# Feed-forward of an encoder: another order of seven block products, early output products in six parts, token sums in four portions, returned operands asked for by thirds

## The chip, the core and the metric

The kernel runs on one core of one Trainium2 chip. The metric is the device time of one execution in microseconds, as the median of several runs. The core has a matrix engine (PE, with its weight loads shown as PEld), three engines for elementwise work (DVE is the vector engine, ACT the scalar engine, POOL the GpSimd engine), and DMA queues; here all loads and stores are issued from SP. Matrix products accumulate in PSUM, in banks of 128 x 512 numbers of 32 bits; everything else is in the on-chip SBUF.

## What is computed

Two layers over 512 tokens of width 1024. Each layer is a feed-forward, a token mixer (neighbourhood attention in the first layer, a bidirectional RWKV-7 scan in the second), and another feed-forward, each followed by a normalization:

```python
D_MODEL = 1024; SEQ = 512; DEPTH = 2; D_FF = 2816; DN_ALPHA = (2 * DEPTH) ** 0.25

def swiglu(x, w_in, w_out):
    gate, up = jnp.split(x @ w_in, 2, axis=-1)
    return (jax.nn.silu(gate) * up) @ w_out

for i in range(DEPTH):
    x = layer_norm(DN_ALPHA * x + 0.5 * swiglu(x, ffn_w_in[i, 0], ffn_w_out[i, 0]), ln_g[i, 0], ln_b[i, 0])
    m = neighbourhood_attention(...) if i % 2 == 0 else rwkv7_bidir(...)
    x = layer_norm(DN_ALPHA * x + m, ln_g[i, 1], ln_b[i, 1])
    x = layer_norm(DN_ALPHA * x + 0.5 * swiglu(x, ffn_w_in[i, 1], ffn_w_out[i, 1]), ln_g[i, 2], ln_b[i, 2])
```

The change is in the feed-forward, which runs four times with other weights.

## The kernel before

**Numbers in two parts.** Every operand of a matrix product is split into a high part (a copy on ACT, line 277, to a shorter format) and a low part (the difference, on DVE or POOL, line 278). A product is three matmuls: high by high, high by low, low by high. So each operand costs one ACT and one DVE or POOL instruction before PE can use it, and a wait of PE for "DVE w L278" is a wait for a low part.

**Blocks.** The inner width of 2816 is 22 blocks f of 128. `ffn()` goes through eleven pairs c, of the blocks f = 2c and 2c + 1. The even blocks, and those up to f = 4, are computed in the ordinary way: 24 matmuls of 512 columns for the gate (`pg`) and 24 for the up part (`pu`), lines 287 to 289, with a bank each; then a silu on ACT (L495) and a product on DVE that reads the bank of `pu` (L497). The odd blocks from f = 5 on (the list `SEVEN`, nine in each feed-forward, 36 in all) go through `Seven.products`.

**The seven products.** This is a Strassen scheme of Winograd's kind with the weights as a 2 x 2 block matrix (gate and up, first and second half of the width) and the tokens' transposed activations as another. `Seven.operands` makes the sums of weight blocks on DVE and splits them: `ua` and `ub` (in the tiles `w`, loaded from `raw`), `one` and `pair` (both in `ring` tiles; L957 and L958 make the sums ahead of these two splits). `Seven.mixes` makes the four sums of token blocks (`right`), once for each feed-forward. Each of the seven products is twelve matmuls of 256 columns (L980). They accumulate in three places: `a` and `f`, which are the two halves of one bank, and `e`, in half of the bank of the block before's `pu`. Partial results go between them by copies on ACT (L972): `copy(e, a)` from bank to bank, `copy(p, f)` to the tile `tmp`. PSUM dependencies are by tile, that is by bank: a matmul into `a` waits for a pending read of `f`, and the other way.

**The output side.** The second matrix is handled by the class `Winograd`. `sums(c)` loads four blocks of the output weights into `ra` (one buffer), makes differences (L1024 to L1027) and splits three of them into `wx`. `early(c - 1)` is a generator of output products X, Z and Y of the pair before, six matmuls of 512 columns each (L1063); `products` takes one part at a time between its own products, by `next(more)`. Of the other operands some (`keep`) stay in ring tiles, some are sent to DRAM (`away`) and returned by `recall`, three loads for each of two streams. When all pairs are done, streams V, Y, Z and Y (`add`) go over the pairs with 6 matmuls of 512 columns for each, with weights that are loaded and split on the way (tiles `w` and `wl`), while DVE adds finished accumulators to x (`more`, L531).

**What sets the order.** PE's order inside `products` is as written (manual schedule for PE); ACT, DVE and POOL are ordered by the scheduler of the framework, and each runs its queue strictly in that order. A wait at the head of a queue stops everything behind it on that engine. `k.behind(first[0])` lets the next product be issued after an instruction given. The tiles named `ring` come from a pool of 11 buffers.

Of the kernel before, what the change touches and what calls it, by code (L numbers as in the profile page):

```python
# [10 lines left out]
F32 = mybir.dt.float32  # L11
# [7 lines left out]
P = 128  # L19
D = 1024  # L20
# [86 lines left out]
class Trunk:  # L107
# [354 lines left out]
    def ffn(self, xT, w_in, w_out, ln, nxt, lead=None):  # L462
# [10 lines left out]
        with self.pool("fa") as pool:  # L473
            out.pool = pool
            keep = [self.ring().rearrange("p (c n i s) -> p c n i s", c=2, n=2, i=2) for _ in range(npairs // 2)]
            keep = [k[:, c] for k in keep for c in range(2)] + [seven.rest.rearrange("p (n i s) -> p n i s", n=2, i=2)]
            for c in range(npairs):
# [3 lines left out]
                for j in range(2):  # L481
# [10 lines left out]
                    if pps:  # L492
# [4 lines left out]
                        nc.vector.scalar_tensor_tensor(dst, halves_of(pu), 0.5, halves_of(s), ALU.mult, ALU.mult)  # L497
                    if f < 2:
                        seven.mixes(f)
# [7 lines left out]
                out.now[c] = pool.tile([P, 2, 3, 256], F32R, name="an", tag="an", bufs=1)  # L507
                self.split(out.now[c][:, 0], out.now[c][:, 1], raw[:, 0:3])
                self.split(keep[c][:, :, 0], keep[c][:, :, 1], raw[:, 3:5])
                tag = ("gbc", "bbc")[c % 2]  # L510
                away = self.home(self.sb).tile([P, 2, 2, 256], F32R, name="away", tag=tag)
                self.split(away[:, :, 0], away[:, :, 1], raw[:, 5:7])
                nc.sync.dma_start(self.away[:, :, c], away.bitcast(F32).rearrange("p n i s -> p n (i s)"))
            params = self.ln_params(ln)
            out.keep = {n: [k[:, n] for k in keep] for n in range(2)}
# [6 lines left out]
        with self.pool("fo") as pool:  # L522
            out.pool = pool
            out.begin(out.t3)
            out.recall(2)
            fin = self.residual_norm(params, nxt)
            hs = (slice(0, 512), slice(512, 1024))
# [16 lines left out]
            for t in (0, 1):  # L544
                more(t, 0, X, ALPHA)
                more(t, 0, V, 1.0, st[t][0])
            out.add("Y", 1, out.t3, range(npairs))
            out.begin(out.b22)
            out.recall(3)
            for t in (2, 3):  # L550
                more(t, 1, Y, 1.0, st[t][1])
            out.add("Z", 2, out.b22, range(npairs), lag=8)
            out.begin(out.t4)
# [337 lines left out]
class Seven:  # L891
# [21 lines left out]
    def mixes(self, part):  # L913

        nc, k = self.nc, self.k
        sub, add = ALU.subtract, ALU.add
        tt = nc.vector.tensor_tensor
        part_of = lambda b, i: b[:, i].bitcast(F32)
        x, y = (k.home(k.sb).tile([P, D], F32, name="mixed", tag=t).rearrange("p (c s) -> p c s", c=4) for t in ("gbc", "bbc"))

        def difference(out, t, a, b):
            tt(out, part_of(a, 0), part_of(b, 0), sub)
            tt(t, part_of(a, 1), part_of(b, 1), sub)
            tt(out, out, t, add)
# [8 lines left out]
        if part:  # L933
            difference(x, y, self.block(1, 1), self.block(0, 1))
            keep(2, x)
        else:
            difference(x, y, self.block(0, 1), self.block(0, 0))
            keep(0, x)
            fold(y, self.block(1, 1), x)
            keep(1, y)  # L940
            fold(x, self.block(1, 0), y)
            keep(3, x)

# [19 lines left out]
    def products(self, f, dst, more):  # L963
# [21 lines left out]
        b, t = self.block, self.right  # L985
        mul(a, ua[:, :, lo], b(0, 0), True)
        copy(e, a)
        next(more)
        with k.behind(first[0]):
            mul(f, ub[:, :, lo], t[0], False)  # L990
        copy(p, f)
        mul(e, self.one, t[1], False)
# [16 lines left out]
class Winograd:  # L1009
# [31 lines left out]
    def early(self, c):  # L1041

        a = self.now.pop(c)
        for name, n, u in zip("XYZ", (0, 2, 1), self.units.pop(c)):
            first = self.banks(name)
            for t in range(2):
                self.product(self.acc[name][t], a[:, :, n], t, u, first, c == NF // 2 - 1)
            yield

    def recall(self, n):  # L1050

        rings = [self.k.ring().rearrange("p (c f) -> p c f", c=4) for _ in range(3)]
        self.keep[n] = []
        for i, r in enumerate(rings):
            m = min(4, NF // 2 - 4 * i)
            self.nc.sync.dma_start(r[:, :m].bitcast(F32), self.k.away[:, n - 2, 4 * i : 4 * i + m])
            self.keep[n] += [r[:, c].rearrange("p (i s) -> p i s", i=2) for c in range(m)]

    def product(self, acc, a, t, u, first, last, more=False):
# [40 lines left out]

    def add(self, name, n, src, cs, lag=None):

# [934 lines left out]
```

## Time and profile before

| what | us |
|---|---|
| median of three runs (2205.87, 2219.66, 2207.17) | 2207.17 |
| the profiled execution, its own time | 2204.32 |
| its span in the trace | 2201.7 |
| mean granted clock of PE in it | 0.991 |

The four feed-forwards lie at about 36 to 345, 600 to 945, 945 to 1305 and 1845 to 2201 us of the span; attention and the scan lie between. The busy time of the engines in these stretches (columns: stretch, its length, then busy us and instructions of PE, PEld, DVE, ACT and POOL, granted clock, busy share of the DMA engines and GB/s):

```profile
36.00:345.00 309.00, 303.74 (x1680) 263.05 (x1679) 227.49 (x331) 141.84 (x210) 30.61 (x11) 1.00 0.58 196
600.00:945.00 345.00, 335.56 (x1905) 292.49 (x1904) 253.39 (x366) 159.32 (x236) 33.97 (x14) 1.00 0.52 180
945.00:1305.00 360.00, 352.67 (x2003) 308.24 (x2002) 269.25 (x396) 166.49 (x253) 49.88 (x22) 1.00 0.55 183
1845.00:2201.00 356.00, 337.73 (x1867) 290.01 (x1865) 257.19 (x373) 158.10 (x235) 30.84 (x12) 0.99 0.52 175
```

PE is busy nearly all the time in all four; DVE is the second. How to read the lines of the profile further on: a group shows engine, line, output and input by the program's names (buffer numbers left out), the shape, its busy time and mean, and the idle time ahead of it with what ended most of that. A line of the timeline shows the start, the duration, the instruction, and in brackets the engine's idle time before it with its releaser. Matmuls are pipelined, so their durations overlap; the pace is read from the starts.

### The profile page before, as it was taken

How to read it: one execution, taken by the hardware profiler on the slowest of the kernel's cores; microseconds unless marked ns; L12 is line 12 of the kernel's file. 1: busy time of each engine (PE TensorE's matmuls, PEld its weight loads, DVE VectorE, ACT ScalarE, POOL GpSimd, SP SyncE). 2: the span in 40 equal slices, each digit the busy share in tenths (PEclk: the TensorE clock that was granted, in tenths of full speed). 3: DMA queues.
4: the chain of work that ended last, by engine and by line, in shares of the span. 5: the costliest groups of instructions: out<-in, count | busy, mean ns of one | idle time of the engine just before them, and what ended most of it. 6: DMA issues, size and time to landing. Idle time of an engine off the chain costs nothing.

```text
span 2201.7 us, 38797 instructions
## 1 busy us (share of the span) xinstructions
PE 2131.1 (97%) x15248; PEld 1726.2 (78%) x15248; DVE 1551.5 (70%) x2506; ACT 1082.2 (49%) x1987; POOL 527.5 (24%) x670
## 2 busy tenths in 40 slices
PE   9999999999999999999999999999998999999998
PEld 8888888887888888787888877446666567788876
DVE  7777767377487777697777779636887558777775
ACT  4444445377344444453444444437776434444443
POOL 1000035555300000520000242046877610000023
PEclk9999999999999999999999999999999999999999
DMA  6544593432334556734555853853544551455583
GB/s 191 174 163 155 177 361 114 117 101 77 113 125 158 159 171 199 298 128 145 159 169 164 311 207 118 293 160 106 135 118 118 169 188 64 152 159 171 163 296 135
DMA packets 160805, 367.81 MB, mean 167 GB/s; under 512 B 32144, under 2 KB 52240, under 8 KB 158576
## 3 DMA queue, kind: packets, MB, share of 16 engines
q1 hardware_dynamic: 160624, 365.36, 50.9%
q8 instruction: 119, 1.95, 0.4%
q14 instruction: 62, 0.51, 0.1%
HBM read 284.29 MB, written 68.94 MB: 160 GB/s over the span
## 4 chain that ended last, share of the span: by engine, by line
PE 63%; DVE 18%; DMA 12%; ACT 3%; issue 2%; POOL 0%; SPq 0%; DVEq 0%; ACTq 0%; POOLq 0%
PE bank L980 13%; PE bank L1063 12%; DMA ra<-in_ffn_w_out_dram 7%; PE a L1255 5%; PE bank L288 5%; PE bank L287 5%; PE bank L289 5%; DVE w L278 4%; PE bank L350 4%; DVE ring L278 2%; ACT w L277 2%; DMA raw<-in_ffn_w_in_dram 2%; PE g L1579 1%; PE y L1255 1%; DVE wx L278 1%
## 5 line engine op out<-in xcount | busy, mean ns | idle before, releaser
L278 POOL TENSOR_TENSOR w<-raw,w 128x1024 fp32r<-128x1024 f32 x38 | 93.4, 2462 | 1206.5 <-ACT w L277 1200.2
L287 PE MATMUL bank<-xT,w 128*128 128x512 f32 x760 | 298.1, 392 | 6.5 <-DVE ar L497 6.5
L278 DVE TENSOR_TENSOR w<-raw,w 128x1024 fp32r<-128x1024 f32 x164 | 200.5, 1223 | 136.4 <-ACT w L277 134.6
L288 PE MATMUL bank<-xT,w 128*128 128x512 f32 x760 | 296.1, 390 | 0.0
L289 PE MATMUL bank<-xT,w 128*128 128x512 f32 x760 | 295.7, 389 | 0.0
L277 ACT ACTIVATE w<-raw 128x1024 fp32r<-128x1024 f32 x202 | 213.0, 1058 | 129.8 <-DMA raw<-in_ffn_w_in_dram 33.6
L1063 PE MATMUL bank<-wx,an 128*128 128x512 f32 x792 | 201.8, 392 | 0.0
L1063 PE MATMUL bank<-w,ring 128*128 128x512 f32 x720 | 171.8, 395 | 7.3 <-DVE w L278 7.3
L287 PEld LDWEIGHTS bank<-xT,w 128*128 128x128 f32 x760 | 142.7, 188 | 37.4 <-DVE ar L497 8.8
L277 ACT ACTIVATE ring<-raw 128x512 fp32r<-128x512 f32 (+1 forms) x99 | 89.3, 904 | 161.5 <-DVE raw L957 119.0
L1063 PEld LDWEIGHTS bank<-w,ring 128*128 128x128 f32 x720 | 136.7, 190 | 38.2 <-DVE w L278 9.0
L289 PEld LDWEIGHTS bank<-xT,w 128*128 128x128 f32 x760 | 142.7, 188 | 30.0
L288 PEld LDWEIGHTS bank<-xT,w 128*128 128x128 f32 x760 | 142.8, 188 | 28.4
L1063 PEld LDWEIGHTS bank<-wx,an 128*128 128x128 f32 x792 | 142.0, 189 | 24.7
L980 PEld LDWEIGHTS bank<-ring,w 128*128 128x128 f32 x864 | 110.8, 191 | 33.4 <-ACT bank L972 30.4
L980 PE MATMUL bank<-ring,w 128*128 128x256 f32 x864 | 119.0, 287 | 15.7 <-ACT bank L972 15.4
L1686 POOL TENSOR_TENSOR tm<-qs,zs 128x126 f32<-128x126 f32 (+22 forms) x248 | 102.8, 414 | 86.9 <-issue 38.9
L1688 POOL TENSOR_TENSOR zs<-zs,tm 128x126 f32<-128x126 f32 (+22 forms) x248 | 112.6, 454 | 19.4
L980 PE MATMUL bank<-ring 128*128 128x256 f32 x864 | 116.3, 284 | 0.1
L980 PEld LDWEIGHTS bank<-ring 128*128 128x128 f32 x864 | 109.6, 193 | 0.4 <-ACT tmp L972 0.4
L495 ACT ACTIVATE tmp<-bank 128x512 f32<-128x512 f32 x52 | 31.1, 597 | 151.8 <-PE bank L289 151.8
L980 PE MATMUL bank<-xT,w 128*128 128x256 f32 x756 | 100.6, 283 | 0.0
(383 smaller groups left out, 4679.4 us busy)
## 6 DMA issues: line engine op xcount, KB each, us to landing
raw<-in_ffn_w_in_dram SPq DMA_DIRECT2D x176, 512.0 KB, 3.7
ra<-in_ffn_w_out_dram SPq DMA_DIRECT2D x44, 1024.0 KB, 5.2
d_away<-away SPq DMA_DIRECT2D x44, 512.0 KB, 4.4
ring<-d_away SPq DMA_DIRECT2D x16, 1024.0 KB, 11.5
xT<-d_late SPq DMA_DIRECT2D x29, 512.0 KB, 8.3
xT<-in_ffn_w_out_dram SPq DMA_DIRECT2D x23, 512.0 KB, 10.0
d_late<-ts SPq DMA_DIRECT2D x44, 256.0 KB, 2.0
d_late<-ra SPq DMA_DIRECT2D x44, 256.0 KB, 2.0
```

Source lines behind the costliest of these rows:

```text
L277: self.hi = self.nc.scalar.activation(h, raw, AF.Copy).ins
L278: self.lo = (eng or self.nc.vector).tensor_tensor(l, raw, h.bitcast(F32), ALU.subtract).ins
L287: nc.tensor.matmul(out, wh, xh, start=start, stop=False)
L288: nc.tensor.matmul(out, wh, xl, start=False, stop=False)
L289: nc.tensor.matmul(out, wl, xh, start=False, stop=stop)
L350: nc.tensor.matmul(acc[t, h], a, u[:, i, h * 512 : (h + 1) * 512], start=first and n == 0, stop=last and n == 2)
L495: nc.scalar.activation(s, pg, AF.Silu)
L980: m = nc.tensor.matmul(out, w[:, i, cs], x[:, j, c], start=start and c + n == 0, stop=c == 3 and n == 2, skip_group_check=True)
L1063: self.nc.tensor.matmul(acc, lhs, u[:, i], start=bool(first) and m == 0, stop=last and m == 2, skip_group_check=more)
L1255: self.nc.tensor.matmul(out[hs], w[:, hs], x, start=start, stop=stop)
L1686: nc.gpsimd.tensor_tensor(tv, qs[:, s, 0:s].rearrange("p (a o) -> p a o", o=1).broadcast_to([P, s, n]), zs[:, s : s + 1, c0:].broadcast_to ...
L1688: nc.gpsimd.tensor_tensor(zs[:, 0:s, c0:], zs[:, 0:s, c0:], tv, ALU.add)
```

## The change

**1. The order of the products.** Before: a (`ua` lo), copy(e, a), one early part of six matmuls, f (`ub` lo), copy(p, f), e (`one`), and so on. After: f (`ub` lo) comes first and opens the bank, copy(p, f), then a (`ua` lo), copy(e, a), three early parts of three matmuls each, e (`one`), and so on; a fourth early part after the sixth product, the other two at the end. `early` now yields after each half of X, Z and Y, so there are six parts of three matmuls in place of three of six.

**2. Token sums.** `mixes` is called at f = 0 to 3 with one portion each, in place of three portions at f = 0 and one at f = 1. Its temporary lies in a ring tile of its own in place of the tags `gbc` and `bbc`. The rings of `keep` are taken as the pairs come and no longer all at the start.

**3. Recall.** `recall` is a generator that issues one of its three loads at a time; `add` asks it at c = 0, 2 and 4. The loads of the norm parameters (`ln_params`) and `residual_norm` now come behind the first Y stream.

All matmuls, splits, copies and DMAs remain, in number and size; lines of the changed file are shifted (980 is 986, 972 is 978, 1063 is 1071, 531 is 532, 495 is 494).

PE in one steady seven, before. The names are tiles with their numbers: bank_457 holds a and f, bank_458 holds e, w_1610 is ua, w_1611 is ub, ring_261 is `one`:

```order
L289 MATMUL bank_458<-xT_93,w_1549 128x512
L980 MATMUL bank_457<-xT_92,w_1610 128x256 [waits Activation_49]
L980 MATMUL bank_457<-xT_92,w_1610 128x256
L980 MATMUL bank_457<-xT_92,w_1610 128x256 [waits DVE_49]
L980 MATMUL bank_457<-xT_92,w_1610 128x256 x9
L1063 MATMUL bank_510<-wx_1304,an_1515 128x512 x2
L1063 MATMUL bank_510<-wx_1304,an_1515 128x512 [waits DVE_49]
L1063 MATMUL bank_511<-wx_1304,an_1515 128x512 x3
L980 MATMUL bank_457<-ring_256,w_1611 128x256 [waits Activation_49]
L980 MATMUL bank_457<-ring_256,w_1611 128x256
L980 MATMUL bank_457<-ring_256,w_1611 128x256 [waits DVE_49]
L980 MATMUL bank_457<-ring_256,w_1611 128x256 x9
```

The same place after (bank_441 holds a and f, w_1605 is ua, w_1606 is ub):

```order
L986 MATMUL bank_441<-ring_256,w_1606 128x256 [waits Activation_49]
L986 MATMUL bank_441<-ring_256,w_1606 128x256
L986 MATMUL bank_441<-ring_256,w_1606 128x256 [waits DVE_49]
L986 MATMUL bank_441<-ring_256,w_1606 128x256 x9
L986 MATMUL bank_441<-xT_92,w_1605 128x256 [waits Activation_49]
L986 MATMUL bank_441<-xT_92,w_1605 128x256 x11
L1071 MATMUL bank_498<-wx_1299,an_1510 128x512 x3
L1071 MATMUL bank_499<-wx_1299,an_1510 128x512 x3
L1071 MATMUL bank_506<-wx_1302,an_1510 128x512 x3
L986 MATMUL bank_442<-ring_257,ring_261 128x256 [waits Activation_49]
```

The f product (of ub) has moved from behind the early part to the front; a's first matmul stands directly behind it and waits for ACT; the early matmuls stand behind a, nine in place of six.

ACT at the same place, before: the silu of the even block, the splits of ub, of `one` and of the pair, then the copies (wx is a split of the output weights):

```order
L495 ACTIVATE tmp_1601<-bank_457 128x512 [waits PE_49]
L277 ACTIVATE w_1611<-raw_1607 128x1024 [waits DMAHW7_49,DVE_49,Activation_49]
L277 ACTIVATE ring_261<-raw_1607 128x512 [waits DVE_49]
L277 ACTIVATE ring_260<-raw_1606 128x1024 [waits DVE_49]
L972 ACTIVATE bank_458<-bank_457 128x256 [waits DVE_49,PE_49]
L277 ACTIVATE wx_1533<-ra_1524 128x512 [waits DMAHW0_49,PE_49]
L972 ACTIVATE tmp_1626<-bank_457 128x256 [waits PE_49]
```

and after:

```order
L494 ACTIVATE tmp_1596<-bank_441 128x512 [waits PE_49]
L277 ACTIVATE w_1606<-raw_1602 128x1024 [waits DMAHW7_49,DVE_49,Activation_49]
L277 ACTIVATE ring_261<-raw_1602 128x512 [waits DVE_49]
L277 ACTIVATE ring_260<-raw_1601 128x1024 [waits DVE_49]
L978 ACTIVATE tmp_1621<-bank_441 128x256 [waits PE_49]
L978 ACTIVATE bank_442<-bank_441 128x256 [waits DVE_49,PE_49]
L277 ACTIVATE wx_1528<-ra_1519 128x512 [waits DMAHW0_49,PE_49]
```

The copy of f to `tmp` now stands directly behind the pair's split (ring_260) and ahead of the copy from bank to bank, which in turn stands ahead of the wx split.

DVE at the start of the V stage of the fourth feed-forward, before (x_17688 to x_17691 are the four token tiles of x):

```order
L531 SCALAR_TENSOR_TENSOR x_17688<-x_17688,bank 128x512 [waits PE_49]
L278 TENSOR_TENSOR w<-xT,w 128x1024 [waits DMAHW5_49,Activation_49]
L531 SCALAR_TENSOR_TENSOR x_17689<-x_17689,bank 128x512 [waits PE_49]
L531 SCALAR_TENSOR_TENSOR x_17688<-x_17688,bank 128x512 [waits DVE_49]
L531 SCALAR_TENSOR_TENSOR x_17690<-x_17690,bank 128x512 [waits PE_49]
...
L531 SCALAR_TENSOR_TENSOR x_17691<-x_17691,bank 128x512
L278 TENSOR_TENSOR wl_20878<-held,wl_20878 128x1024 [waits DMAHW4_49,DMAHW1_49,Activation_49]
L531 SCALAR_TENSOR_TENSOR x_17689<-x_17689,bank 128x512
L278 TENSOR_TENSOR w<-held,w 128x512 [waits DMAHW7_49,Activation_49]
```

and after:

```order
L532 SCALAR_TENSOR_TENSOR x_17679<-x_17679,bank 128x512 [waits PE_49]
L532 SCALAR_TENSOR_TENSOR x_17680<-x_17680,bank 128x512 [waits PE_49]
L532 SCALAR_TENSOR_TENSOR x_17681<-x_17681,bank 128x512 [waits PE_49]
L278 TENSOR_TENSOR w<-xT,w 128x1024 [waits DMAHW7_49,Activation_49]
L532 SCALAR_TENSOR_TENSOR x_17679<-x_17679,bank 128x512 [waits DVE_49]
...
L278 TENSOR_TENSOR wl_20862<-held,wl_20862 128x1024 [waits DMAHW5_49,DMAHW1_49,Activation_49]
L532 SCALAR_TENSOR_TENSOR x_17682<-x_17682,bank 128x512 [waits DVE_49]
L532 SCALAR_TENSOR_TENSOR x_17682<-x_17682,bank 128x512
L532 SCALAR_TENSOR_TENSOR x_17680<-x_17680,bank 128x512
L278 TENSOR_TENSOR w<-held,w 128x512 [waits DMAHW7_49,Activation_49]
```

Three updates of x in place of one stand ahead of the split of `w<-xT`, and three in place of one between the split of `wl` and the last split of `w<-held`.

The diff, cut to its core:

```diff
@@ ffn
-            keep = [self.ring().rearrange("p (c n i s) -> p c n i s", c=2, n=2, i=2) for _ in range(npairs // 2)]
-            keep = [k[:, c] for k in keep for c in range(2)] + [seven.rest.rearrange("p (n i s) -> p n i s", n=2, i=2)]
+            keep = []
...
-                    if f < 2:
+                    if f < 4:
                         seven.mixes(f)
...
+                if c == npairs - 1:
+                    keep.append(seven.rest.rearrange("p (n i s) -> p n i s", n=2, i=2))
+                elif c % 2 == 0:
+                    two = self.ring().rearrange("p (c n i s) -> p c n i s", c=2, n=2, i=2)
+                    keep += [two[:, 0], two[:, 1]]
...
-            params = self.ln_params(ln)
...
-            out.recall(2)
-            fin = self.residual_norm(params, nxt)
...
-            out.add("Y", 1, out.t3, range(npairs))
+            out.add("Y", 1, out.t3, range(npairs), back=out.recall(2))
+            params = self.ln_params(ln)
+            fin = self.residual_norm(params, nxt)
             out.begin(out.b22)
-            out.recall(3)
...
-            out.add("Z", 2, out.b22, range(npairs), lag=8)
+            out.add("Z", 2, out.b22, range(npairs), lag=8, back=out.recall(3))
@@ Seven.mixes
-        x, y = (k.home(k.sb).tile([P, D], F32, name="mixed", tag=t).rearrange("p (c s) -> p c s", c=4) for t in ("gbc", "bbc"))
+        if part == 0:
+            self.mixed = [h.rearrange("p (c s) -> p c s", c=4) for h in flat2(k.ring(F32))]
+        x, y = self.mixed
...
@@ Seven.products
-        mul(a, ua[:, :, lo], b(0, 0), True)
+        mul(f, ub[:, :, lo], t[0], True)
+        copy(p, f)
+        with k.behind(first[0]):
+            mul(a, ua[:, :, lo], b(0, 0), False)
         copy(e, a)
-        next(more)
-        with k.behind(first[0]):
-            mul(f, ub[:, :, lo], t[0], False)
-        copy(p, f)
+        for _ in range(3):
+            next(more)
         mul(e, self.one, t[1], False)
@@ Winograd.early
             for t in range(2):
                 self.product(self.acc[name][t], a[:, :, n], t, u, first, c == NF // 2 - 1)
-            yield
+                yield
@@ Winograd.recall
-        rings = [self.k.ring().rearrange("p (c f) -> p c f", c=4) for _ in range(3)]
         self.keep[n] = []
-        for i, r in enumerate(rings):
+        for i in range(3):
+            r = self.k.ring().rearrange("p (c f) -> p c f", c=4)
             m = min(4, NF // 2 - 4 * i)
             self.nc.sync.dma_start(r[:, :m].bitcast(F32), self.k.away[:, n - 2, 4 * i : 4 * i + m])
             self.keep[n] += [r[:, c].rearrange("p (i s) -> p i s", i=2) for c in range(m)]
+            yield
@@ Winograd.add
             if c % 2 == 0:
                 now = (src.__name__, c)
+                next(iter(back), None)
```

More of the change, by code (lines that the diff above doesn't have):

```diff
@@ L931, in keep @@
             k.split(self.right[n][:, 0], self.right[n][:, 1], t)
-        if part:
+        if part == 0:
+            difference(x, y, self.block(0, 1), self.block(0, 0))
+            keep(0, x)
+        elif part == 1:
+            fold(y, self.block(1, 1), x)
+            keep(1, y)
+        elif part == 2:
+            fold(x, self.block(1, 0), y)
+            keep(3, x)
+        else:
             difference(x, y, self.block(1, 1), self.block(0, 1))
             keep(2, x)
[L936 to L942, printed above, removed]
     def operands(self, f):
@@ L1099, in begin, with add @@
             self.begun[src.__name__, c] = self.load(src, c, False)
-    def add(self, name, n, src, cs, lag=None):
+    def add(self, name, n, src, cs, lag=None, back=()):
         first = self.banks(name)
```

## The prediction

> **What bounds the kernel now.** I read the page first (busy shares, the chain that ended last), then the waits of the matmul engine, then one pair of blocks in the timeline, engine by engine. The lines of the page and of the waits:
>
> ```profile
> PE 2131.1 (97%) x15248; PEld 1726.2 (78%) x15248; DVE 1551.5 (70%) x2506; ACT 1082.2 (49%) x1987; POOL 527.5 (24%) x670
> ...
> PE bank L980 13%; PE bank L1063 12%; DMA ra<-in_ffn_w_out_dram 7%; PE a L1255 5%; PE bank L288 5%; PE bank L287 5%; PE bank L289 5%; DVE w L278 4%; PE bank L350 4%; DVE ring L278 2%; ACT w L277 2%; DMA raw<-in_ffn_w_in_dram 2%; PE g L1579 1%; PE y L1255 1%; DVE wx L278 1%
> ...
> L980 PEld LDWEIGHTS bank<-ring,w 128*128 128x128 f32 x864 | 110.8, 191 | 33.4 <-ACT bank L972 30.4
> L980 PE MATMUL bank<-ring,w 128*128 128x256 f32 x864 | 119.0, 287 | 15.7 <-ACT bank L972 15.4
> ```
>
> ```profile
> PE bank L980 <- ACT bank L972: 15.4, 26, 2.6
> PE a L1255 <- DMA wv<-in_w_rv_dram: 8.9, 4, 3.4
> PE bank L1063 <- DVE w L278: 7.3, 4, 3.8
> PE bank L287 <- DVE ar L497: 6.5, 7, 1.3
> ```
>
> PE is busy for 97% of the span, so only what stands in PE's own queue counts: its waits and its matmuls. The change leaves the matmuls as they are, 84 for each seven. The largest wait is that of L980 for the ACT copy at L972; it is the wait the change goes at. Its weight loads idle 30.4 us for that copy over the 36 sevens. Here is one seven of the first feed-forward, PE, then ACT, then DVE (start, us, what, idle before it and its releaser):
>
> ```profile
> 150.15 0.39 PE L289 MATMUL bank<-xT,w 128*128 128x512 f32 x1
> 150.38 1.59 PE L980 MATMUL bank<-xT,w 128*128 128x256 f32 x12
> 151.81 1.55 PE L1063 MATMUL bank<-wx,an 128*128 128x512 f32 x6
> 153.72 1.70 PE L980 MATMUL bank<-ring,w 128*128 128x256 f32 x12 [0.37 <-ACT bank L972]
> 155.26 1.60 PE L980 MATMUL bank<-ring 128*128 128x256 f32 x12
> 156.70 1.48 PE L980 MATMUL bank<-xT,w 128*128 128x256 f32 x11
> ...
> 151.44 1.06 ACT L277 ACTIVATE ring<-raw 128x1024 fp32r<-128x1024 f32 x1 [0.57 <-DVE raw L958]
> 153.30 0.37 ACT L972 ACTIVATE bank<-bank 128x256 f32<-128x256 f32 x1 [0.81 <-DVE ar L497]
> 153.58 0.62 ACT L277 ACTIVATE wx<-ra 128x512 fp32r<-128x512 f32 x1
> 155.46 0.38 ACT L972 ACTIVATE tmp<-bank 128x256 f32<-128x256 f32 x1 [1.25 <-PE bank L980]
> ...
> 147.77 1.22 DVE L278 TENSOR_TENSOR w<-raw,w 128x1024 fp32r<-128x1024 f32 x1
> 150.72 0.69 DVE L958 TENSOR_TENSOR raw<-raw 128x512 f32<-128x512 f32 x1
> 152.52 0.69 DVE L497 SCALAR_TENSOR_TENSOR ar<-bank,tmp 128x512 f32<-128x512 f32 x1
> ```
>
> Read it so. PE does a at 150.38 and an early part at 151.81, then waits: f needs copy(e,a), that copy needs L497 to have read bank e, and L497 ends at 152.52 + 0.69 = 153.21. The pace from the rows: twelve matmuls of 256 columns take 156.70 - 155.26 = 1.44, so 0.12 each, and a 512-column one 150.38 - 150.15 = 0.23. Without the wait f would start at 151.81 + 6 x 0.23 = 153.2; it starts at 153.72, so the wait costs 0.5. After a wait the next twelve take 155.26 - 153.72 = 1.54, a restart of 0.10. Summed by start times over the 36 sevens I get 25 us, of it 0.50 in each of 31 steady ones; the rest is in the first sevens of the second to fourth feed-forward.
>
> **The change part by part. 1: f goes first, in the steady sevens.** What is gained is the 0.50 above: copy(e,a) now stands behind nine early matmuls, 9 x 0.23 = 2.07 us, and L497 is done before it is asked for. That cover is enough.
>
> What is added: a's first matmul writes the bank that copy(p,f) still reads, and nothing stands between f and a. The parts of the turn are all in the rows. f's last matmul starts 11 x 0.12 = 1.32 after its first and takes 0.28 (1.59 less 1.32, rounded); the copy follows 0.04 later (155.46 against 155.14 + 0.28); and from the start of a copy to PE's next matmul it is 153.72 - 153.30 = 0.42. So a can start 1.32 + 0.28 + 0.04 + 0.42 = 2.06 after f, against 1.44 without a wait: 0.62, with the restart 0.72. That is the least it can cost.
>
> ACT may be later than that. In its queue the pair's split (151.44 above) stands ahead of copy(p,f), and it ends at 152.50, that is 2.12 after the seven began, while f is over at 1.60. The next ACT instruction begins 0.09 before the one ahead ends (153.58 against 153.30 + 0.37). So a starts at 2.12 - 0.09 + 0.42 = 2.45; less 1.44 plus 0.10, the new wait is 1.11 here. Two more sevens, the ones where that split comes earliest and nearly latest among the steady ones:
>
> ```profile
> 818.17 1.59 PE L980 MATMUL bank<-xT,w 128*128 128x256 f32 x12
> 818.80 1.06 ACT L277 ACTIVATE ring<-raw 128x1024 fp32r<-128x1024 f32 x1 [0.57 <-DVE raw L958]
> ...
> 843.47 1.59 PE L980 MATMUL bank<-xT,w 128*128 128x256 f32 x12
> 844.80 1.06 ACT L277 ACTIVATE ring<-raw 128x1024 fp32r<-128x1024 f32 x1 [0.57 <-DVE raw L958]
> ```
>
> The split ends 1.69 after the start in the one and 2.39 in the other; the mean over the 31 is 2.0. The new waits are 0.72 (the least), 1.36, and 1.04 at the mean, where I allow 0.05 for a start of the chain that shifts. Net + 0.54 each, times 31: **+ 16.7**. The ends: + 0.22 each if ACT is never late (+ 7), and + 0.86 each (+ 27) if all are as at 843. I take the mean, since nothing in the change moves L958 or the split against the end of the seven before.
>
> f also needs the low part of ub, which DVE ended at 147.77 + 1.22 = 148.99, 1.39 before the seven. Taken the same way this margin is never under 1 in a steady seven, so f isn't late: 0. The six-part early stream has the same matmuls at other places: 0; its cover is that each part is twelve or more matmuls behind its operands.
>
> The Trainium skill, PSUM — Partial Sum Buffer, Summary: rules for kernel authors, asks that a matmul target another bank than the one being read, with semaphores by bank. The kernel's a and f are halves of one bank, so this rule speaks against f followed at once by a; the 0.42 after the copy in the rows agrees with it. By a reading in which halves were free of each other the 16.7 would be - 15.5.
>
> **2: first sevens and token sums.** Rows of the second and third feed-forward, and the granted clock (after PE busy, PEld, DVE, ACT and POOL):
>
> ```profile
> 649.37 0.50 PE L287 MATMUL bank<-xT,w 128*128 128x512 f32 x1 [0.97 <-DVE ar L497]
> 657.27 0.50 PE L287 MATMUL bank<-xT,w 128*128 128x512 f32 x1 [0.72 <-DVE ar L497]
> 666.71 1.45 PE L980 MATMUL bank<-ring,w 128*128 128x256 f32 x10 [2.30 <-ACT bank L972]
> ...
> 657.14 1.21 DVE L278 TENSOR_TENSOR w<-raw,w 128x1024 fp32r<-128x1024 f32 x1
> ...
> 1022.54 2.26 PE L980 MATMUL bank<-ring,w 128*128 128x256 f32 x12 [2.40 <-ACT bank L972]
> ...
> 1023.00:1027.00 4.00, 4.00 (x23) 4.00 (x22) 0.48 (x1) 0.38 (x1) 0.00 (x0) 0.57 0.84 296
> ```
>
> Smaller token sums let L497 go ahead of them on DVE, so the 0.97 and 0.72 shrink, and the 2.30 goes. But f now waits for the low part of ub, 657.14 + 1.21 = 658.35; with the new order PE is ready for it some 2.0 earlier. Then copy(p,f) stands behind the splits: about 1.5. Removed 4.4 with restarts, added 2.0 + 1.5 and some 0.6 left before: near 0 for each of three feed-forwards, between - 1 and + 2. In the first feed-forward I take 0. The second seven of the second one is counted like a steady one: + 0.5. The third one runs four microseconds at a clock of 0.57 after its idle 2.40, which costs 1.7; two idles of 2.0 and 1.5 could bring it or spare it, so 0, with 1.7 either way in each. The Trainium skill, TensorE: Matmul & The Clock Gate, Part 1, has half clock only after an idle window of about 3.4 us; the row differs, since 2.40 was enough, and by the page alone no startup would lose anything here. Sum **+ 0.5**.
>
> **3: recall by thirds, norm parameters later.** The three loads of returned operands are the same, issued from SP at c = 0, 2 and 4 of the stream ahead of the one that uses them. A stream is eleven blocks of six matmuls, 66 x 0.23 = 15 us; a load takes 11.5 by the first row below, so it lands in time: 0. What moves is DVE's queue in the V stage, here of the fourth feed-forward:
>
> ```profile
> ring<-d_away SPq DMA_DIRECT2D x16, 1024.0 KB, 11.5
> ...
> 2143.64 6.32 PE L1063 MATMUL bank<-w,ring 128*128 128x512 f32 x14 [3.77 <-DVE w L278]
> ...
> 2129.39 2.65 DVE L278 TENSOR_TENSOR w<-xT,w 128x1024 fp32r<-128x1024 f32 x1
> 2131.97 6.06 DVE L531 SCALAR_TENSOR_TENSOR x<-x,bank 128x512 f32<-128x512 f32 x10
> 2137.95 2.88 DVE L278 TENSOR_TENSOR wl<-held,wl 128x1024 fp32r<-128x1024 f32 x1
> 2141.35 2.23 DVE L278 TENSOR_TENSOR w<-held,w 128x512 fp32r<-128x512 f32 x1
> ...
> 2128.57 2.40 POOL L278 TENSOR_TENSOR w<-held,w 128x1024 fp32r<-128x1024 f32 x1
> 2137.34 2.40 POOL L278 TENSOR_TENSOR w<-held,w 128x1024 fp32r<-128x1024 f32 x1 [6.38 <-ACT w L277]
> ...
> 2143.00:2150.00 7.00, 6.37 (x15) 0.51 1.00 386
> ```
>
> The wait of 3.77 is DVE's queue, in which three splits that stood beside a POOL split took 2.65, 2.88 and 2.23 instead of the 1.22 of the row at 147.77 (twice) and 0.69 for half the width: 4.6 too much. In the new order two more x updates stand ahead of the first and three behind the second, so the first begins as POOL's ends, the second before POOL's next; only the third still meets it, for some 1.6. So - 3.0, and the 7 us at a clock of 0.51 behind it (3.4 lost) go too, as the short idle at 153.72 is followed by full pace. In the other three feed-forwards the same wait is (7.3 - 3.8) / 3 = 1.2, with no POOL split beside; half an x update more ahead of the split (6.06 / 10 = 0.6) costs + 0.3 each, an estimate. Sum 0.9 - 3.0 - 3.4 = **- 5.5**, between - 6.4 (nothing added) and + 3 (each wait 0.75 longer). The Trainium skill, SBUF — State Buffer, Who interferes with whom, has a VectorE operation with two SBUF inputs and a GpSimd operation shut each other out, the second waiting for all of the first; the rows agree.
>
> **Sum.** 16.7 + 0.5 - 5.5 = + 11.7, on the profiled execution's 2204.3: 2216. The median of the runs shown is 2207.2, 2.9 above it; on that it is 2219.
>
> **The rivals.**
> A, ACT is never late: only the turn of 0.72 is paid. For it: the split ends by 1.7 in some sevens. Against: 2.0 at the mean. Then 7 + 0.5 - 5.5 = + 2: 2209.
> B, slower: f waits. The sums' operand ra has one buffer; its chain sets both ub's low part and the pair's split. copy(e,a) now stands on ACT ahead of the first split of ra, about 1 us later than at 153.58. If that delay reached the next load of ra, the split would end later by it, and each 0.1 costs 3.1 us; past 0.3 (which gives 2219 + 10) it decides. Against it: the last of ra's three splits waits for PE at the seven's end either way. With 0.3 to 0.8: 2229 to 2244.
> C, the change does what it says: PE finds copy(p,f) done and all waits for copies go: - 15.5 - 5.5 and some 4 in the first sevens (three times 1.5), 2182. Against it: the wait of a for that copy has no matmul ahead of it.
>
> **How the numbers follow.** The forecast 0.58, A 0.15, B 0.22, C 0.05. A measurement of this kernel tells about 1% from no change, 2185 to 2229. The forecast, between its ends, lies within it, A too; B lies above, with 0.02 of the forecast's upper end; C is below. So faster 0.05, same 0.71, slower 0.24. The range: down to 2203, below A by the - 6 of the first sevens and the clock; up to 2235, a third of the way into B; outside it are C and the longer half of B.
>
> **What would show it.** In the new profile: L980's waits for the copy into the bank are gone, and PE's waits for the copy into tmp sum to some 25 to 35 us; the pair's split ends around + 2.0 and the copy follows at once. The last V wait is about 1 and the clock stays full after it. What would make it wrong: steady sevens as near to each other on the mean as these two now come at best (843.47 - 818.17 = 25.30), or f idle for ub.

## The result, and the profile after

| | us, median (lowest to highest), runs |
|---|---|
| before | 2206.52 (2203.28 to 2219.66), 4 |
| after | 2231.77 (2229.34 to 2240.67), 4 |
| ratio of after to before, 95% interval | 1.0115 (1.0077 to 1.0152) |

The changed kernel is 25 us slower. Its profiled execution took 2240.67 us, the longest of its four; a second profile of the same program (e0_change below) shows which part of that is the execution's own.

The page of the kernel after, and its longest waits of PE (waited for, us in total, times, longest):

```profile
PE 2140.8 (96%) x15248; PEld 1737.6 (78%) x15248; DVE 1540.5 (69%) x2506; ACT 1087.1 (49%) x1987; POOL 521.3 (23%) x670
...
L986 PE MATMUL bank<-xT,w 128*128 128x256 f32 x756 | 110.1, 298 | 40.7 <-ACT tmp L978 40.7
```

```profile
PE bank L986 <- ACT tmp L978: 40.7, 36, 2.3
...
PE bank L1071 <- DVE w L278: 4.6, 5, 1.3
...
PE bank L287 <- DVE ar L496: 2.5, 4, 0.7
PE bank L986 <- ACT tmp L1002: 2.4, 3, 1.5
```

The wait for the copy into bank e, 15.4 us before, is gone from the list. In its place stands the copy of f to `tmp`, 40.7 us in all 36 sevens. The waits behind L496 went from 6.5 to 2.5 and those for the splits in the V stage from 7.3 to 4.6. One steady seven in the timeline, PE, ACT and DVE:

```profile
178.32 1.59 PE L986 MATMUL bank<-ring,w 128*128 128x256 f32 x12
180.93 1.69 PE L986 MATMUL bank<-xT,w 128*128 128x256 f32 x12 [1.02 <-ACT tmp L978]
182.46 2.23 PE L1071 MATMUL bank<-wx,an 128*128 128x512 f32 x9
184.52 1.60 PE L986 MATMUL bank<-ring 128*128 128x256 f32 x12
...
179.54 1.06 ACT L277 ACTIVATE ring<-raw 128x1024 fp32r<-128x1024 f32 x1 [0.57 <-DVE raw L964]
180.50 0.37 ACT L978 ACTIVATE tmp<-bank 128x256 f32<-128x256 f32 x1
182.66 0.37 ACT L978 ACTIVATE bank<-bank 128x256 f32<-128x256 f32 x1 [1.78 <-PE bank L986]
...
175.27 0.69 DVE L1031 TENSOR_TENSOR ts<-ra 128x512 f32<-128x512 f32 x1 [2.10 <-DMA ra<-in_ffn_w_out_dram]
175.88 1.22 DVE L278 TENSOR_TENSOR w<-raw,w 128x1024 fp32r<-128x1024 f32 x1
178.82 0.69 DVE L964 TENSOR_TENSOR raw<-raw 128x512 f32<-128x512 f32 x1
```

f runs at once. Its last matmul is over 1.6 us after 178.32, but ACT is in the pair's split until 180.60 and the copy comes at 180.50. PE resumes at 180.93, 0.43 after the copy's start: a starts 2.61 after f instead of 1.44. The copy into e finds its cover of nine early matmuls and costs nothing.

To see where the time went I matched the matmuls of the two traces by their order and took how far the starts moved apart in each part of the four feed-forwards: up to the end of the first seven, the steady sevens, and the V stage with what follows. "Rest" is attention, the scan and the norms.

| moved against the profile of before, us | first sevens | steady sevens | V stage on | rest | all |
|---|---|---|---|---|---|
| after | + 3.7 | + 35.7 | - 6.2 | + 2.9 | + 36.1 |
| e0_change (the same kernel again) | + 3.6 | + 30.4 | - 5.9 | - 8.9 | + 19.2 |
| e1_order | + 0.2 | + 25.6 | - 4.7 | - 2.6 | + 18.6 |
| e2_rest | - 6.5 | + 2.5 | - 1.7 | - 7.1 | - 12.8 |
| e3_between | - 4.7 | - 13.9 | - 7.5 | - 8.1 | - 34.1 |
| e4_a_first_9 | - 9.3 | - 3.6 | + 10.1 | - 5.1 | - 7.9 |
| e5_pair_late | - 4.4 | + 15.0 | + 15.7 | - 2.3 | + 24.0 |
| e6_one_between | - 4.5 | - 12.8 | - 8.3 | - 6.0 | - 31.5 |
| e8_between_alone | - 6.0 | - 14.5 | - 6.8 | + 1.4 | - 26.0 |
| e9_pair_late_v_dve | - 4.3 | + 18.4 | - 8.9 | - 8.2 | - 2.9 |

The rest differs by up to 12 us between two executions of the same program (in the scan: waits for small DMAs, and five stretches of 4 us at a clock of 0.51 to 0.57 in the first profile against one in e0_change); that is why one profile says + 36 or + 19 and the medians + 25 or + 19. The loss is in the steady sevens, and the V stage gives some of it back.

Three of the steady sevens are worse than the others. The one at 860:

```profile
860.84 1.46 PE L986 MATMUL bank<-ring,w 128*128 128x256 f32 x10 [0.49 <-DVE w L278]
864.61 1.65 PE L986 MATMUL bank<-xT,w 128*128 128x256 f32 x6 [2.31 <-ACT tmp L978]
...
858.96 0.69 DVE L1031 TENSOR_TENSOR ts<-ra 128x512 f32<-128x512 f32 x1 [4.16 <-DMA ra<-in_ffn_w_out_dram]
```

Here the load of ra took 7.1 us (asked for at 851.82) where others take 5. DVE waits 4.16 for it, and everything behind it, ub's low part and the pair's split, is late by that. This seven and the one at 2013 cost about 3 us each, and so does the one at 698, the second of the second feed-forward, whose load took 6.5 us. About half of that is no wait: behind each of the three lies a stretch with the clock at 0.57 to 0.60 over 4 us (703 to 707, 864 to 868, 2017 to 2021), and a with its early parts takes 4.9 to 5.2 us there instead of 3.6.

The V stage of the fourth feed-forward, PE and DVE, and the stretch behind it:

```profile
2182.57 3.53 PE L1071 MATMUL bank<-w,ring 128*128 128x512 f32 x14 [0.70 <-DVE w L278]
...
2173.55 1.42 DVE L278 TENSOR_TENSOR w<-xT,w 128x1024 fp32r<-128x1024 f32 x1
2178.48 1.21 DVE L278 TENSOR_TENSOR wl<-held,wl 128x1024 fp32r<-128x1024 f32 x1
2181.41 1.10 DVE L278 TENSOR_TENSOR w<-held,w 128x512 fp32r<-128x512 f32 x1
...
2182.00:2190.00 8.00, 7.43 (x32) 6.02 (x33) 3.04 (x6) 2.21 (x3) 5.02 (x2) 1.00 1.02 413
```

The three splits take 1.42, 1.21 and 1.10 us, the wait is 0.70, and the clock stays at 1.00.

### The profile page after: what moved, and what is told of

It is laid out like the page before. It is cut to its first block, busy times and chain, and to the rows that moved or that the text cites. A ratio compares the mean times of both kernels' runs of the same rounds, so it can differ in the third digit from the quotient of the medians.

```text
span 2237.8 us, 38812 instructions
## 1 busy us (share of the span) xinstructions
PE 2140.8 (96%) x15248; PEld 1737.6 (78%) x15248; DVE 1540.5 (69%) x2506; ACT 1087.1 (49%) x1987; POOL 521.3 (23%) x670
## 4 chain that ended last, share of the span: by engine, by line
PE 65%; DVE 16%; DMA 11%; ACT 4%; issue 3%; SPq 0%; DVEq 0%; POOL 0%; ACTq 0%; POOLq 0%
PE bank L1071 14%; PE bank L986 13%; DMA ra<-in_ffn_w_out_dram 7%; PE a L1264 5%; PE bank L288 4%; PE bank L287 4%; PE bank L289 4%; DVE w L278 4%; PE bank L350 4%; ACT w L277 2%; DVE x L532 1%; DVE ring L278 1%; PE g L1588 1%; PE y L1264 1%; DMA wv<-in_w_rv_dram 1%
## 5 line engine op out<-in xcount | busy, mean ns | idle before, releaser
L287 PEld LDWEIGHTS bank<-xT,w 128*128 128x128 f32 x760 | 142.7, 188 | 32.8 <-issue 3.1
L289 PEld LDWEIGHTS bank<-xT,w 128*128 128x128 f32 x760 | 142.6, 188 | 29.9
L288 PEld LDWEIGHTS bank<-xT,w 128*128 128x128 f32 x760 | 142.8, 188 | 28.5
L278 DVE TENSOR_TENSOR wx<-ra,wx 128x512 fp32r<-128x512 f32 x132 | 89.9, 689 | 97.5 <-ACT wx L277 97.3
L986 PE MATMUL bank<-xT,w 128*128 128x256 f32 x756 | 110.1, 298 | 40.7 <-ACT tmp L978 40.7
L986 PEld LDWEIGHTS bank<-xT,w 128*128 128x128 f32 x756 | 99.7, 200 | 48.1 <-ACT tmp L978 48.1
L277 ACT ACTIVATE wx<-ra 128x512 fp32r<-128x512 f32 x132 | 81.2, 627 | 108.7 <-PE bank L1071 102.8
```

The source lines that it names most:

```text
L277: self.hi = self.nc.scalar.activation(h, raw, AF.Copy).ins
L278: self.lo = (eng or self.nc.vector).tensor_tensor(l, raw, h.bitcast(F32), ALU.subtract).ins
L287: nc.tensor.matmul(out, wh, xh, start=start, stop=False)
L288: nc.tensor.matmul(out, wh, xl, start=False, stop=False)
L289: nc.tensor.matmul(out, wl, xh, start=False, stop=stop)
L986: m = nc.tensor.matmul(out, w[:, i, cs], x[:, j, c], start=start and c + n == 0, stop=c == 3 and n == 2, skip_group_check=True)
```

## The experiments

My theory: the loss is a's wait for copy(p,f), which has no matmul ahead of it and is made longer by the pair's split on ACT. The rivals: the token sums, the rings or the recall cost the time; or f first is late whatever stands behind it. "Before" in each result is the kernel before, timed beside it on the same chip; the chip is not the same for all experiments.

**e1_order, the order alone.** The kernel before with this, and `early` yielding after each half:

```diff
-        mul(a, ua[:, :, lo], b(0, 0), True)
-        copy(e, a)
-        next(more)
-        with k.behind(first[0]):
-            mul(f, ub[:, :, lo], t[0], False)
-        copy(p, f)
+        mul(f, ub[:, :, lo], t[0], True)
+        copy(p, f)
+        with k.behind(first[0]):
+            mul(a, ua[:, :, lo], b(0, 0), False)
+        copy(e, a)
+        for _ in range(3):
+            next(more)
```

> The kernel before with the new order of the products and the six early parts alone; token sums, rings, recall and norm parameters as before. Theory (the loss is a's uncovered wait for copy(p,f) in the sevens): as slow as the whole change, 2222 to 2236 us, with PE's waits for that copy summing to about 40 us. Rival (the token sums in a ring of their own, or the recall by thirds, cost the time at the startups): under 2215 us.

2223.25 against 2201.21 us, ratio 1.0103 (1.0073 to 1.0134). PE's waits for the copy sum to 33.5 us, a little under the 40 expected. The order alone makes the loss; the rival falls.

**e2_rest, all but the order.** The changed kernel with a, copy(e, a), six early matmuls, f, copy(p, f).

> The changed kernel with the old order of the products (a, copy(e,a), six early matmuls, f); token sums in portions, lazy rings, recall by thirds stay. Theory: the steady wait is the old 0.5 us each, the fourth feed-forward's V wait shrinks, so 2195 to 2206 us. Rival: above 2215 us, if the other parts carry the loss.

2198.45 against 2201.21 us, ratio 0.9978 (0.9959 to 0.9996). The other parts gain 3 us, in the first sevens (- 6.5 in the table), where L496 no longer waits behind the token sums. So they are a small gain, and the two results add up to what the whole change does: + 22 and - 3 against + 19 for e0_change. One thing missed: I expected the V wait of the fourth feed-forward to shrink, and it is the old 3.8 us again. DVE has its old order there. The first two lines are this run, with one update of x ahead of the split as before; the third is e1_order, with three:

```profile
2117.27 0.69 DVE L532 SCALAR_TENSOR_TENSOR x<-x,bank 128x512 f32<-128x512 f32 x1 [4.19 <-PE bank L1072]
2117.87 3.00 DVE L278 TENSOR_TENSOR w<-xT,w 128x1024 fp32r<-128x1024 f32 x1
...
2154.25 1.88 DVE L531 SCALAR_TENSOR_TENSOR x<-x,bank 128x512 f32<-128x512 f32 x3 [4.94 <-PE bank L1064]
```

This run has the recall by thirds and e1_order has not, and e1_order has the short wait (0.62). So the new order of DVE in the V stage comes with the new places of the products and early parts, and not with the recall.

**e3_between, cover between f and a.**

```diff
         copy(p, f)
+        for _ in range(2):
+            next(more)
         with k.behind(first[0]):
             mul(a, ua[:, :, lo], b(0, 0), False)
         copy(e, a)
-        for _ in range(3):
+        for _ in range(2):
             next(more)
```

> The changed kernel with two of the early parts (six matmuls, 1.36 us) moved between f and a, and two instead of three behind a. Theory: the copy ends at about +2.28 - 0.09 + 0.42 = 2.61 us after the seven's start, f and the early matmuls last 1.44 + 1.36 = 2.80, so the steady wait is about 0 and the time 2185 to 2200 us. Rival (f first is itself late, by the low part of ub, whatever stands behind it): no better than 2215 us.

2169.98 against 2201.21 us, ratio 0.9858 (0.9825 to 0.9890), the fastest of all and below my range of 2185 to 2200: beside the steady sevens (- 13.9) the first sevens and the V stage gain too (- 4.7 and - 7.5). The rival falls: f first is no loss when something stands between f and a. The same place as above, PE and ACT, and the split of ub on DVE:

```profile
148.08 1.59 PE L986 MATMUL bank<-ring,w 128*128 128x256 f32 x12
149.51 1.55 PE L1073 MATMUL bank<-wx,an 128*128 128x512 f32 x6
150.90 1.59 PE L986 MATMUL bank<-xT,w 128*128 128x256 f32 x12
...
148.08 1.06 ACT L277 ACTIVATE ring<-raw 128x1024 fp32r<-128x1024 f32 x1 [0.57 <-DVE raw L964]
149.71 0.38 ACT L978 ACTIVATE tmp<-bank 128x256 f32<-128x256 f32 x1 [0.56 <-PE bank L986]
...
144.42 1.23 DVE L278 TENSOR_TENSOR w<-raw,w 128x1024 fp32r<-128x1024 f32 x1 [1.48 <-ACT w L277]
145.56 0.68 DVE L1033 TENSOR_TENSOR ts<-ra 128x512 f32<-128x512 f32 x1
```

No row of PE has an idle time. A second thing has changed, which I had not meant: the scheduler now puts the low part of ub ahead of the first sum of ra on DVE, so the pair's split ends 1.06 us after the seven's start and no longer 2.3. Is it the cover or this that helps? The wait of 0.72 for the turn alone would be there without cover; e6 has less cover with the same order on DVE, e5 an early copy without cover.

**e4_a_first_9, the old order with more cover.** The changed kernel with a, copy(e, a), three parts (nine matmuls), f, copy(p, f).

> The changed kernel with a first again, and nine early matmuls (2.04 us) in place of six between a and f. Theory: copy(e,a) is done about 3.35 us after the seven's start, a and the early matmuls last 1.44 + 2.04 = 3.48, so the old wait of 0.5 us goes too: 2183 to 2195 us. Rival (the 0.5 us isn't a lack of cover, the chain behind L496 moves along with it): within 4 us of e2_rest.

2199.25 against 2201.21 us, ratio 0.9996 (0.9978 to 1.0014): a miss. The number came out as the rival said, but not for its reason. f does start without a wait, and another product waits. PE's row, then two of ACT:

```profile
157.38 1.69 PE L986 MATMUL bank<-ring 128*128 128x256 f32 x12 [0.78 <-ACT tmp L978]
...
156.00 1.06 ACT L277 ACTIVATE w<-raw 128x1024 fp32r<-128x1024 f32 x1 [1.86 <-DMA raw<-in_ffn_w_in_dram]
156.96 0.36 ACT L978 ACTIVATE tmp<-bank 128x256 f32<-128x256 f32 x1
```

ACT stands 1.86 us at a split whose load has not come, with the copy of the `one` product queued behind it; that product was over at 155.0 plus 0.2. The scheduler put the split first. So the steady sevens gain only - 3.6, and the V stage, where waits for POOL's splits appear, loses 10.1.

**e0_change, the changed kernel again, and three that go with it.**

> The changed kernel once more, as the measure for the three that follow: 20 to 28 us above the kernel before. Its first profile had two sevens (at 860 and 2013 us) whose load of ra took 7 us in place of 5; theory: those are single late loads, so this profile shows the steady pattern in all or nearly all sevens and some 6 us less of waits. Rival: they stand at the same places again.

2223.97 against 2204.98 us, ratio 1.0095 (1.0080 to 1.0110). The waits for the copy are 34.9 us, 5.8 less. The seven at 2013 is an ordinary one here; that at 860 is late again, by less (its split ends 3.0 us after the start, not 4.3). e1_order has a late one near 1996, the same block as the one at 2013. So these loads are late in some executions and not in others, at a few places; why there was not tried.

**e5_pair_late, the pair's split behind the copy.**

```diff
-        k.split(self.pair[:, 0], self.pair[:, 1], raws[0])
...
-        copy(p, f)
+        with k.behind(copy(p, f).ins):
+            k.split(self.pair[:, 0], self.pair[:, 1], two)
```

> The changed kernel, with the pair's split held behind copy(p,f) in ACT's queue; nothing else moves. Theory (the split ahead of the copy makes part of the new wait): the steady wait falls from about 1.27 us (2.28 - 0.09 + 0.42 - 1.44 + 0.10) to the turn alone, 0.72, so 31 x 0.55 = 17 us less than e0_change: 4 to 11 us above the kernel before. Rival (the wait is the turn from PE to ACT and back, the split is only beside it): 20 us above or more.

2228.12 against 2204.98 us, ratio 1.0118 (1.0095 to 1.0140). The time is as the rival has it; the trace is not. The steady wait did fall to the turn alone, and the gain was given back in the V stage. PE's waits, then a steady seven:

```profile
PE bank L985 <- ACT tmp L977: 18.2, 39, 0.5
PE bank L1071 <- DVE w L278: 17.0, 8, 3.8
```

```profile
176.53 1.59 PE L985 MATMUL bank<-ring,w 128*128 128x256 f32 x12
178.60 1.69 PE L985 MATMUL bank<-xT,w 128*128 128x256 f32 x12 [0.47 <-ACT tmp L977]
```

a starts 2.07 after f (2.06 was the turn in the prediction), and the waits for the copy halve, 18.2 against 34.9. In the first feed-forward a starts 2.06 or 2.07 us after f in each of the eight steady sevens, against 2.41 to 2.98 in e0_change. But the wait in the V stage is now 3.8 in all four feed-forwards. In the first, DVE, then POOL, then the stretch behind it with the granted clock:

```profile
314.32 3.17 DVE L278 TENSOR_TENSOR wl<-xT,wl 128x1024 fp32r<-128x1024 f32 x1
317.42 2.82 DVE L278 TENSOR_TENSOR w<-xT,w 128x512 fp32r<-128x512 f32 x1
...
314.01 2.40 POOL L278 TENSOR_TENSOR w<-xT,w 128x1024 fp32r<-128x1024 f32 x1 [5.05 <-ACT w L277]
316.79 2.90 POOL L278 TENSOR_TENSOR w<-xT,w 128x1024 fp32r<-128x1024 f32 x1 [0.38 <-ACT w L277]
...
320.00:324.00 4.00, 3.71 (x10) 2.98 (x11) 2.14 (x6) 1.06 (x1) 0.00 (x0) 0.58 1.01 423
```

The DVE splits begin while POOL splits run and end 1.08 and 0.55 us after those (317.49 against 316.41, 320.24 against 319.69), a little less than the 1.22 and 0.69 that such splits take alone. DVE's order has changed too: five updates of x stand ahead of the first split and seven ahead of the one of `wl`. The table has the balance: 30.4 - 15.0 = 15 us gained in the steady sevens, where 17 were expected, and 21.6 lost in the V stage.

**e9_pair_late_v_dve, the same without POOL in the V stream.**

```diff
-        k.split(u[:, 0], u[:, 1], raw, k.nc.vector if c % 4 else k.nc.gpsimd)
+        k.split(u[:, 0], u[:, 1], raw, k.nc.vector if c % 4 or src == self.b21 else k.nc.gpsimd)
```

> As e5_pair_late, with the splits of the V stream's weights all on DVE, none on POOL. In e5_pair_late PE waits 3.8 us in each V stage, behind two DVE splits that take 3.17 and 2.82 us beside POOL splits. Theory (the two engines shut each other out, and that is what gave back e5's gain in the sevens): the two DVE splits return to 1.2 and 0.7 us, the wait falls to about 3.8 - 4.1 + 2.4 (two more splits in DVE's queue) = 2 us or less, and the half clock behind it goes: 10 to 20 us less than e5_pair_late. Rival (DVE's queue is late for another reason, its own length): the two more splits make the wait 5 to 6 us, and the time no better than e5_pair_late.

2202.49 against 2200.46 us, ratio 1.0008 (0.9991 to 1.0026): 21 us better than e5_pair_late against the same kernel before (+ 2.0 and + 23.1). The V stage goes from + 15.7 to - 8.9. PE's waits there:

```profile
PE bank L1071 <- DVE w L278: 2.2, 4, 0.6
```

0.6 at most where 3.8 stood, though DVE has more splits to do; so the rival falls. The two DVE splits in the first feed-forward:

```profile
310.67 1.22 DVE L278 TENSOR_TENSOR wl<-xT,wl 128x1024 fp32r<-128x1024 f32 x1
...
313.60 2.60 DVE L278 TENSOR_TENSOR w<-xT,w 128x512 fp32r<-128x512 f32 x1
```

The first is back at 1.22, without a POOL split beside it; the second still takes 2.60, beside a POOL split of the next stream (313.25 to 315.65). It ends at 316.20 and not at 320.24. Of these 4.0 us some 2.2 are the shorter splits (3.17 + 2.82 against 1.22 + 2.60). The other 1.8 are three updates of x, which the scheduler has moved behind the last split, so this run doesn't show the conflict alone. The clock is 1.00 over the 4 us behind it.

**e6_one_between, less cover.** As e3_between with one part (three matmuls) between f and a, three behind a, none ahead of the last product.

> As e3_between with one early part (three matmuls, 0.68 us) between f and a, three behind a, none before the last product, two at the end. The low part of ub stands ahead of the sums of ra on DVE here as in e3_between, where the pair's split ended 1.06 us after the seven's start. Theory: then the copy is done at 2.06 us, f and the part last 2.12, the wait is under 0.1: as fast as e3_between, 25 to 33 us below the kernel before. Rival (the split ends at 2.28 as in the change, and only the longer cover of e3_between hid that): a wait of 0.6, some 12 us below.

2173.76 against 2204.98 us, ratio 0.9880 (0.9848 to 0.9911), the same as e3_between within the intervals. Its split ends 1.06 us after the start, and a starts 2.13 after f (200.42 against 198.29), as the cover of 1.44 + 0.68 allows. Three matmuls are enough if the copy isn't held up.

**e8_between_alone, e3's order in the kernel before.** The order of e3_between put into the kernel before, with its own token sums, rings and recall.

> The kernel before with the product order of e3_between and six early parts alone; token sums, rings, recall and norm parameters as before. Theory (the other parts are worth the 3 to 6 us that e2_rest showed, and add up): 25 to 28 us below the kernel before. Rival (the order needs the other parts, since the first sevens lose without them): less than 18 us below.

2175.05 against 2204.98 us, ratio 0.9870 (0.9853 to 0.9887), 30 us below the kernel before and so a little better than I expected. The order with cover needs nothing else of the change. The medians of e3_between and this run are 31 and 30 us below; their intervals overlap, so whether the other parts add their 3 us here can't be told.

## Why the prediction was right, and where it was too small

The prediction was + 12 us with a range to 2235; measured are + 25 and, on another chip (e0_change), + 19. The mechanism was right, and one term too small. The median of 2232 lies just above the forecast's own upper end (2229), and within the range because that reaches into the stretch of rival B.

- **The old wait goes, the cover of nine matmuls is enough.** Right: no wait for the copy into bank e is left.
- **The turn of 0.72.** Right. e5_pair_late shows it alone: 2.06 or 2.07 from f to a in all 32 sevens behind the first ones, which is 0.72 with the restart of 0.10.
- **The pair's split ahead of the copy.** Right in kind: e5_pair_late removes 15 us by moving it. The Trainium skill's rule on banks (PSUM — Partial Sum Buffer, Summary: rules for kernel authors) pointed the right way too: a after f in the same bank waits in every seven.
- **The size, + 16.7 for the steady sevens.** This is the step that was off: + 35.7 and + 30.4 (first profile and e0_change). From f to the third product it is 1.44 + 1.44 + 9 x 0.23 = 4.95 us without a wait. By the starts, the new wait is 1.23 at the median of 32 sevens and 1.52 at the mean in the first profile, and 1.12 and 1.26 in e0_change, where I had 1.04; the old wait, read the same way, was 0.51. So 32 sevens lose 32 x 0.75 = 24 us in e0_change and 32 x 1.01 = 32 in the first profile, which had more late loads of ra (about 3 us each, half of it the low clock behind the wait). The remainder is in the last seven of each feed-forward: waits for L1002 (2.4 and 4.2 us in all), and in e0_change one more stretch at low clock, 0.61 in 2140 to 2144. I hadn't seen either.
- **What moved the split.** In the median seven the pair's split ends 2.26 and 2.14 us after the start (2.00 before), and not at the 2.05 that I had allowed. I had said that nothing in the change moves the chain against the seven ahead. But the load of ra is asked for 8.13 us ahead of the seven and no longer 8.47, because the low part of the last split of the ra before (`wx`) ends later by that. DVE's rows at the end of the pair before, first of the kernel before (its seven starts at 176.11), then of the kernel after (178.32):

```profile
165.19 1.23 DVE L278 TENSOR_TENSOR w<-raw,w 128x1024 fp32r<-128x1024 f32 x1
166.33 0.69 DVE L278 TENSOR_TENSOR ring<-ar,ring 128x512 fp32r<-128x512 f32 x1
...
167.39 1.22 DVE L278 TENSOR_TENSOR w<-raw,w 128x1024 fp32r<-128x1024 f32 x1 [0.21 <-ACT w L277]
168.53 0.42 DVE L503 TENSOR_TENSOR ar<-ar 128x256 f32<-128x256 f32 x1
168.87 0.68 DVE L278 TENSOR_TENSOR ring<-ar,ring 128x512 fp32r<-128x512 f32 x1
```

The low part of `wx` is next in both. A difference of `ar` (L503) now stands between the splits, where it stood ahead of both before, and 168.87 - 168.53 is the 0.34. It is so in all 32 sevens of both traces of the change, and in none of the kernel before.
- **Rival B** had this chain, and its condition came true: a delay of 0.3 us in the load's request (0.34). Its reason did not: on ACT the last split of ra ends 9.92 us ahead of the seven in both kernels (medians), so copy(e,a) ahead of the splits isn't what delays it. Nor does f wait, but for the first sevens and single late ones.
- **First sevens, + 0.5.** Measured + 3.6. The waits came out as forecast: in the second feed-forward f waits 2.0 (in two pieces), a 1.8 and the block ahead 0.8, against 4.5 in all before. What I took as 0 is the clock. Behind these waits all of the later three feed-forwards have a stretch at a low clock, where before only the third had one. Here the fourth after, in windows of 4 us (the last numbers are the granted clock, the DMA share and GB/s):

```profile
1932.00:1936.00 4.00, 1.83 (x12) 1.63 (x13) 3.51 (x6) 1.96 (x3) 0.00 (x0) 0.98 0.40 129
1936.00:1940.00 4.00, 4.00 (x18) 3.68 (x17) 0.90 (x2) 1.33 (x2) 0.00 (x0) 0.59 0.70 224
```

4.00 us at 0.59 cost 1.6, and this comes in two feed-forwards more than before; I had allowed 1.7 either way in each and taken 0.
- **The V stage, - 5.5.** Measured - 6.2 and - 5.9, nearly all in the fourth feed-forward; wait 0.70, full clock. The reading of DVE's order was right: e2_rest has the old order on DVE and the old wait. That I put it under the recall by thirds was wrong, since e1_order has it without that. In the other three feed-forwards I had no POOL split beside and + 0.9 in all. POOL splits do stand beside there (before, the last DVE split of the first V stage takes 2.27 us at 311.21, and POOL is busy from 309.60 to 315.74), and the three waits sum to 3.6 after 3.5. That splits on DVE and POOL hold each other up agrees with the Trainium skill (SBUF — State Buffer, Who interferes with whom), which adds that the order of issue decides who waits.
- **Recall by thirds, token sums, rings: 0.** Right within 3 us.

What wasn't tried: what in the new order makes the scheduler move L503, why some loads of ra take 7 us, and the changed order with ub's low part ahead of ra on DVE but without cover.

## What to carry to other kernels

A wait is hidden only by work between the producer and its consumer on the waiting engine: moving the cover from one pair to the next bares the first, and three to six matmuls at the right place were worth 1.2 to 1.4% here. When two accumulators share a bank, a read of one is a wait for the other; put other work behind the reader. And an edit in one stage can change the order that the scheduler gives another, and with it shift that stage into a conflict or out of it (here DVE against POOL, a wait of 3.8 us and a stretch at low clock each time), so compare two traces stage by stage before a change is called useless.

## What the runs showed of the hardware

A DVE split that takes 1.22 us alone took 3.17 us when it began while a POOL split ran, and one of 0.69 took 2.82; they ended 1.08 and 0.55 us after the POOL splits (e5_pair_late). PE ran at a clock of 0.58 for some four microseconds after an idle of 3.8 us, and at 0.59 after a window of 4 us in which it was busy for 1.83 and no single wait was over 1.9 us. The Trainium skill (TensorE: Matmul & The Clock Gate, Part 1) has a low clock only after an idle window of about 3.4 us; by these runs several shorter waits close together can be enough. They aren't always: in the kernel before, PE was busy for 1.42 us of 1902 to 1906, and the clock of the next 4 us was 1.00. Two executions of one program differ by up to 12 us outside the feed-forwards, half of what this change moves.
